# Expert products of two blocks interleaved over two PSUM banks

## The chip, the cores and the metric

The kernel runs on one core of a Trainium2 chip. The metric is the device time of one execution in microseconds; the time of a kernel is the median of its runs. The engines are TensorE (PE; its weight loads are shown apart as PEld), VectorE (DVE), ScalarE (ACT), GpSimd (POOL) and SyncE (SP), which here issues most of the transfers between HBM and the on-chip memory. PSUM is the memory that the matmuls write: eight banks, each of which takes one result of 128x512 float32.

## What is computed

A two-layer transformer block in float32 over 256 tokens and 256 context tokens. Each layer is a mixing part (a long convolution, a Fourier mix and differential attention) and then a feed-forward part with 16384 small experts, of which each token uses 128. The change is in that last part:

```python
def peer(t, wq, keys, u, v):
    ...                                        # top-k over 8 heads gives indices idx and gates g
    def chunk(args):
        tc, ic, gc = args
        hid = jnp.einsum('td,tkd->tk', tc, u[ic])
        return jnp.einsum('tk,tkd->td', gc * jax.nn.gelu(hid, approximate=False), v[ic])
```

Layer 0 runs it for 512 tokens, layer 1 for 256. Every `u` and `v` has 16384 rows of 1024.

## The kernel before

**Dense experts.** The kernel does not gather the experts of a token. It goes over all 16384 in 128 blocks of 128 and takes a gate of zero for those that a token does not use. For a block `b` it forms the hidden values of 128 experts for all `n` tokens (the hidden product, `u` transposed times the tokens), applies Gelu, multiplies by the gates, and adds the product with the block's 128 rows of `v` (the value product) onto sums that stay in PSUM over all 128 blocks. In layer 0, 384 tokens are done in this way; the other 128 tokens' rows are gathered by POOL with indirect transfers and summed on DVE (`junk`, lines 1067, and `acc`, 1077), four 128x1024 rows of each pass per pair of blocks, into a pool `row` of three buffers. In layer 1 all 256 tokens are done densely.

**Split floats.** Each float32 operand is split into two float32r parts (line 105, `split`): ACT casts it to the high part (`wh`, `vh`, `ah`), DVE subtracts that and writes the low part (`wl`, `vl`, `al`). `mm3` (line 100) then issues three matmuls, high times high, high times low and low times high. A hidden product is 8 chunks of 1024 / 128 times three matmuls, 24 in all, into one PSUM bank. A value product is, for each 128 tokens `tt` and each half (512) of the 1024 columns, three matmuls.

**Pairs.** Blocks go in pairs (`SB = 2`). `stage1` makes a block's gated hidden values (`a`, then `ah` and `al`), `stage2` splits the pair's rows of `v` and issues the value products of both blocks. In program order, hidden products of a pair stand ahead of the value products of the pair before it, so PE alternates: hidden of pair k, values of pair k-1, hidden of k+1, values of k. The accumulators `pacc` take 2n/128 banks, one for each `tt` and half: six in layer 0, four in layer 1. The value loop before is half by half, and in a half over `tt`, with both blocks in the innermost loop: six matmuls into one bank, then the next.

**Prefilled blocks.** 32 blocks of each layer (blocks 0 and 1 of every eight) have their hidden values made earlier, beside the routing, and stored in HBM (`Hd`). For these pairs `stage1` only loads `a` from `Hd`. PE then has no hidden products for that pair, and the value products of two pairs stand back to back. This comes up 15 times in each layer, and once more behind the last pair. It is called a crossing below.

**Buffers.** `vh` and `vl` have four buffers each, one for each half and block of a pair; `wh` and `wl` have three, `ha` (the tile `a`) three, the raw tiles `w` six and `wv` three.

**What sets the order.** The tile framework reorders the instructions of each engine by its own estimate of when they become ready, within the data's dependencies; on the chip each engine then runs its queue in order, and waits at semaphores. The sums over gathered rows are pinned to program order among themselves.

The names above are those in the rows and in the profile: `pm` and `pa` are PSUM tiles, `th` and `tl` the tokens' two parts, `gt` the gates.

Of the kernel before, what the change touches and what calls it, by code (L numbers as in the profile page):

```python
# [9 lines left out]
F32 = mybir.dt.float32  # L10
# [11 lines left out]
P = 128  # L22
L = 256
NT = 512
NG = 128
# [24 lines left out]
def tile_dit(ctx, tc, A, out, dbg=None):  # L50
# [36 lines left out]
    def pmt(shape=(P, 512)):  # L87
        return pm.tile(list(shape), F32, tag="pm", name=nm("pm"))
# [49 lines left out]
    def wraw(src):  # L138
        w = w4.tile([P, 1024], F32, tag="w4", name=nm("w4"))
        nc.sync.dma_start(w, src)  # L140
        return w

    def wsplit(src, eng=None):
        hi = whp.tile([P, 1024], F32R, tag="wh", name=nm("wh"))
        lo = whp.tile([P, 1024], F32R, tag="wl", name=nm("wl"))
        split(hi, lo, src, eng)
        return hi, lo
# [605 lines left out]
    def exact(o, w, xf):  # L753
        for c in range(8):
            mm(o, w[:, c * P:(c + 1) * P], xf[:, c], c == 0, c == 7)

    def hidden(l, n, b, th, tl, xf=None):
        w = wraw(A["u"][l, b])
        ps = pmt()
        if xf is not None:  # L760
            exact(ps[:, :n], w, xf)
        else:
            uh, ul = wsplit(w)
            for c in range(8):
                cs = slice(c * P, (c + 1) * P)
                mm3(ps[:, :n], uh[:, cs], ul[:, cs], th[:, c, :n], tl[:, c, :n], c == 0, c == 7)
        a = scope["ha"].tile([P, 512], F32, tag="a", name=nm("a"))
        S.activation(a[:, :n], ps[:, :n], AF.Gelu)
        return a

    NPRE = (32, 32)
    HEAD_FILLS = ((0, 1, 1, 1, 2, 2, 2, 8), (0, 1, 1, 1, 1, 1, 1, 8))
# [4 lines left out]

    def prefill(l, n, npre, th, tl, xf, Hd):
        for k in range(npre):
            a = hidden(l, n, PRE_BLOCK[l][k], th, tl, xf)  # L780
            nc.scalar.dma_start(Hd[k, :, :n], a[:, :n])
            yield

    def experts(l, n, npre, th, tl, Gd, Hd, acc, hook):
        nq = n // 32
        pacc = [pat() for _ in range(4)] + [pmt() for _ in range(n // P * 2 - 4)]
        gt = [None]

        def stage1(b):
            if b % GB == 0:  # L790
                gt[0] = b16t((P, 16, GB, 32), name="gt")
                nc.sync.dma_start(gt[0][:, :nq], Gd[:, :nq, b:b + GB, :])
            if b in PRE_BLOCK[l]:
                k = PRE_BLOCK[l].index(b)
                a = scope["ha"].tile([P, 512], F32, tag="a", name=nm("a"))
                nc.sync.dma_start(a[:, :n], Hd[k, :, :n])
            else:
                a = hidden(l, n, b, th, tl)
            a3 = a[:, :n].rearrange("p (q k) -> p q k", k=32)
            V.tensor_tensor(a3, a3, gt[0][:, :nq, b % GB], ALU.mult)  # L800
            ah, al = tagged("ah", F32R, 4), tagged("al", F32R, 4)
            split(ah[:, :n], al[:, :n], a[:, :n])
            return ah, al

        def stage2(b0, blocks):
            ws = []
            for i in range(SB):
                w = scope["ex"].tile([P, 1024], F32, tag="wv", name=nm("wv"), bufs=3)
                nc.sync.dma_start(w, A["v"][l, b0 + i])
                ws.append(w)  # L810
            vs = {}
            for half in range(2):
                for i in range(SB):
                    vh, vl = tagged("vh", F32R, 4), tagged("vl", F32R, 4)
                    split(vh, vl, ws[i][:, half * 512:(half + 1) * 512])
                    vs[half, i] = vh, vl
            end = b0 + SB == P
            for half, tt in ([(h, t) for t in range(n // P) for h in range(2)] if end else
                             [(h, t) for h in range(2) for t in range(n // P)]):
                ts = slice(tt * P, (tt + 1) * P)  # L820
                for i, (ah, al) in enumerate(blocks):
                    vh, vl = vs[half, i]
                    mm3(pacc[tt * 2 + half], ah[:, ts], al[:, ts], vh, vl, b0 == 0 and i == 0, end and i == SB - 1)

        prev = None
        for b0 in range(0, P, SB):
            cur = [stage1(b0 + i) for i in range(SB)]
            if prev is not None:
                stage2(b0 - SB, prev)
            prev = cur  # L830
            hook(b0 // SB)
        stage2(P - SB, prev)

        def result(s):
            rows = []
            for tt in range(2 * s, min(2 * s + 2, n // P)):
                y = scope["ex"].tile([P, 1024], F32, tag="wv", name=nm("y"), bufs=3)
                S.copy(y[:, 0:512], pacc[tt * 2])
                V.tensor_copy(y[:, 512:1024], pacc[tt * 2 + 1])
                rows.append(y)  # L840
            if len(rows) < 2:
                rows.append(acc[:, 0:2].rearrange("p a b -> p (a b)"))
            return rows

        return result
# [375 lines left out]
```

## Time and profile before

| | |
|---|---|
| median of 3 runs | 3024.02 us (3019.01 to 3027.01) |
| profiled execution | 3018.95 us, span 3017.2 us |
| mean granted clock of TensorE | 0.978 of full speed |
| PE, PEld busy | 2864.0 us (95%), 2435.9 us (81%) |
| DVE, ACT, POOL busy | 2223.2 us (74%), 1247.6 us (41%), 700.7 us (23%) |
| expert stage of layer 0 | 875 to 1860 us of the span |
| expert stage of layer 1 | 2380 to 3017 us of the span |

Busy time of PE counts a matmul from its start to its modelled end, and matmuls overlap; the distance between two starts says what one costs. On ACT and DVE, too, an instruction can begin some 0.08 us before the modelled end of the one ahead of it. A wait is put down to the releaser that came last.

### The profile page before, as it was taken

How to read it: one execution, taken by the hardware profiler on the slowest of the kernel's cores; microseconds unless marked ns; L12 is line 12 of the kernel's file. 1: busy time of each engine (PE TensorE's matmuls, PEld its weight loads, DVE VectorE, ACT ScalarE, POOL GpSimd, SP SyncE). 2: the span in 40 equal slices, each digit the busy share in tenths (PEclk: the TensorE clock that was granted, in tenths of full speed). 3: DMA queues.
4: the chain of work that ended last, by engine and by line, in shares of the span. 5: the costliest groups of instructions: out<-in, count | busy, mean ns of one | idle time of the engine just before them, and what ended most of it. 6: DMA issues, size and time to landing. Idle time of an engine off the chain costs nothing.

```text
span 3017.2 us, 43660 instructions
## 1 busy us (share of the span) xinstructions
PE 2864.0 (95%) x15976; PEld 2435.9 (81%) x15976; DVE 2223.2 (74%) x4464; ACT 1247.6 (41%) x2294; POOL 700.7 (23%) x609
## 2 busy tenths in 40 slices
PE   6889999999989999999999999899799999999999
PEld 2678778776667888888898897788788898899888
DVE  7766786797977887888887787746688657765665
ACT  3334565421443333333333334336414455555554
POOL 4544433430013333333333332300200000000000
PEclk8899999999999999999999999999999999999999
DMA  7323555233788898889888885225457977766662
GB/s 261 108 97 116 175 180 220 101 114 105 278 332 326 315 326 300 307 318 323 312 317 300 307 312 186 81 97 176 165 162 250 331 249 243 259 223 223 221 224 103
DMA packets 234536, 682.19 MB, mean 226 GB/s; under 512 B 21956, under 2 KB 92682, under 8 KB 231120
## 3 DMA queue, kind: packets, MB, share of 16 engines
q1 hardware_dynamic: 172080, 505.48, 48.4%
q0 software_dynamic: 38928, 140.35, 13.1%
q10 hardware_dynamic: 23312, 33.56, 3.1%
q8 instruction: 125, 2.05, 0.3%
q14 instruction: 91, 0.75, 0.1%
HBM read 612.20 MB, written 67.11 MB: 225 GB/s over the span
## 4 chain that ended last, share of the span: by engine, by line
PE 52%; issue 15%; DVE 14%; DMA 13%; POOL 4%; ACT 2%; POOLq 0%; DVEq 0%; SPq 0%; ACTq 0%
PE pm L98 32%; PE pa L98 19%; DMA row<-in_ug_dram,ix 7%; DMA row<-in_v_dram,ix 4%; DVE og L734 3%; POOL row L1049 2%; DVE wl L110 1%; DVE oa L730 1%; DVE junk L171 1%; DVE acc L1077 1%; DVE junk L1067 1%; DVE vl L110 1%; POOL qt L466 0%; DMA a<-Hd 0%; POOL pr L167 0%
## 5 line engine op out<-in xcount | busy, mean ns | idle before, releaser
L98 PE MATMUL pm<-th,wh 128*128 128x256 f32 (+2 forms) x1680 | 532.4, 317 | 2.3 <-DVE th L241 2.3
L98 PE MATMUL pm<-tl,wh 128*128 128x256 f32 (+2 forms) x1680 | 530.2, 316 | 3.3 <-DVE tl L242 3.2
L98 PE MATMUL pm<-th,wl 128*128 128x256 f32 (+2 forms) x1680 | 529.7, 315 | 0.7 <-DVE wl L110 0.7
L106 ACT CAST wh<-w 128x1024 fp32r<-128x1024 f32 x328 | 343.0, 1047 | 409.3 <-PE pm L98 351.1
L110 DVE TENSOR_TENSOR wl<-w,wh 128x1024 fp32r<-128x1024 f32 x312 | 392.5, 1259 | 161.5 <-ACT wh L106 160.7
L98 PE MATMUL pa<-vl,ah 128*128 128x512 f32 x1024 | 406.1, 397 | 26.5 <-DVE vl L110 26.5
L110 DVE TENSOR_TENSOR vl<-wv,vh 128x512 fp32r<-128x512 f32 x512 | 339.1, 687 | 119.2 <-ACT vh L106 113.6
L106 ACT CAST vh<-wv 128x512 fp32r<-128x512 f32 x512 | 305.3, 619 | 265.4 <-PE pm L98 86.0
L98 PE MATMUL pa<-vh,ah 128*128 128x512 f32 x1024 | 402.5, 394 | 5.1 <-ACT vh L106 5.1
L98 PE MATMUL pa<-vh,al 128*128 128x512 f32 x1024 | 403.7, 394 | 0.3 <-DVE al L110 0.3
L98 PE MATMUL pm<-acc,w 128*128 128x256 f32 (+1 forms) x1280 | 355.6, 427 | 8.6 <-ACT acc L1011 8.6
L98 PEld LDWEIGHTS pm<-tl,wh 128*128 128x128 f32 x1680 | 320.9, 191 | 13.6 <-DVE tl L242 4.5
L98 PEld LDWEIGHTS pm<-th,wh 128*128 128x128 f32 x1680 | 321.0, 191 | 11.8 <-DVE th L241 2.9
L98 PEld LDWEIGHTS pm<-th,wl 128*128 128x128 f32 x1680 | 320.8, 191 | 5.4 <-DVE wl L110 0.9
L106 ACT CAST ah<-a 128x384 fp32r<-128x384 f32 (+1 forms) x256 | 117.7, 460 | 439.5 <-DVE a L800 399.6
L98 PEld LDWEIGHTS pm<-acc,w 128*128 128x128 f32 x1280 | 235.8, 191 | 78.0 <-ACT acc L1011 9.0
L1049 POOL DMA_INDIRECT row<-in_ug_dram,ix x128 | 165.3, 1291 | 507.7 <-DVE junk L1067 298.5
L98 PEld LDWEIGHTS pa<-vl,ah 128*128 128x128 f32 x1024 | 194.7, 190 | 70.5 <-DVE vl L110 32.7
L1049 POOL DMA_INDIRECT row<-in_v_dram,ix x128 | 170.6, 1332 | 311.5 <-DVE acc L1077 279.3
L98 PEld LDWEIGHTS pa<-vh,ah 128*128 128x128 f32 x1024 | 194.5, 190 | 44.8 <-ACT vh L106 6.3
L98 PEld LDWEIGHTS pa<-vh,al 128*128 128x128 f32 x1024 | 194.7, 190 | 41.1 <-DVE al L110 0.8
L1077 DVE SCALAR_TENSOR_TENSOR acc<-row,gg,acc 128x1024 f32<-128x1024 f32 x127 | 162.8, 1282 | 62.7 <-DMA row<-in_v_dram,ix 61.8
(309 smaller groups left out, 5292.5 us busy)
## 6 DMA issues: line engine op xcount, KB each, us to landing
w<-in_u_dram SPq DMA_DIRECT2D x256, 512.0 KB, 4.2
wv<-in_v_dram SPq DMA_DIRECT2D x256, 512.0 KB, 4.9
w<-in_w_ada_dram SPq DMA_DIRECT2D x96, 512.0 KB, 4.3
w<-in_w_in_dram SPq DMA_DIRECT2D x88, 512.0 KB, 3.8
Gd<-st SPq DMA_DIRECT2D x18, 2048.0 KB, 7.2
gt<-Gd SPq DMA_DIRECT2D x16, 1536.0 KB, 10.6
w<-in_wq_dram SPq DMA_DIRECT2D x32, 512.0 KB, 3.6
gt<-Gd SPq DMA_DIRECT2D x16, 1024.0 KB, 6.7
```

Source lines behind the costliest of these rows:

```text
L98: T.matmul(o, l, r, start=start, stop=stop, skip_group_check=True)
L106: S.copy(hi, src)
L110: (eng or V).tensor_tensor(lo[:, ks], src[:, ks], hi[:, ks].bitcast(F32), ALU.subtract)
L171: i = V.scalar_tensor_tensor(slot((P, 1024), BF16, "junk"), w, 1.0, sil[:, s], op0=ALU.mult, op1=ALU.mult, accum_out=m)
L730: V.tensor_tensor(oa, row(0), iob, ALU.is_equal)
L734: V.tensor_tensor(og[:, w * HG:(w + 1) * HG], oa, gv[:, w * HG:(w + 1) * HG, None].to_broadcast([P, HG, P, 2]), ALU.mult)
L1049: nc.gpsimd.indirect_dma_start(out=r, out_offset=None, in_=src, in_offset=bass.IndirectOffsetOnAxis(ap=ix, axis=0))
L1067: pin(V.scalar_tensor_tensor(slot((P, 1024), BF16, "junk"), r, 1.0, ta, op0=ALU.mult, op1=ALU.mult, accum_out=hg[:, k:k + 1]))
L1077: pin(V.scalar_tensor_tensor(ta, r, gg[:, k:k + 1], ta, op0=ALU.mult, op1=ALU.add))
```

## The change

The hidden products of a pair are issued together by `hidden_pair`: for each chunk and each of the three parts, first the matmul of one block, then that of the other, so that consecutive matmuls write two PSUM banks in turn. Both Gelus stand behind the pair. Prefilled blocks keep the old form (`hidden`). In `stage2` the loop over `tt` is now outermost and the two halves are innermost: for each block and each of the three parts, a matmul into the bank of half 0, then one into that of half 1. The numbers of matmuls, weight loads, casts, subtractions and transfers stay the same.

```diff
-    def hidden(l, n, b, th, tl, xf=None):
...
+    def hidden_pair(l, n, b, th, tl):
+        us = [wsplit(wraw(A["u"][l, b + i])) for i in range(SB)]
+        ps = [pmt() for i in range(SB)]
+        for c in range(8):
+            cs = slice(c * P, (c + 1) * P)
+            for k, (w, t) in enumerate(((0, th), (0, tl), (1, th))):
+                for i in range(SB):
+                    mm(ps[i][:, :n], us[i][w][:, cs], t[:, c, :n], c == 0 and k == 0, c == 7 and k == 2)
+        return [gelu(n, p) for p in ps]
...
+        def raw(b0):
+            if b0 not in PRE_BLOCK[l]:
+                return hidden_pair(l, n, b0, th, tl)
+            r = []
+            for i in range(SB):
+                a = scope["ha"].tile([P, NT - NG], F32, tag="a", name=nm("a"))
+                nc.sync.dma_start(a[:, :n], Hd[PRE_BLOCK[l].index(b0 + i), :, :n])
+                r.append(a)
+            return r
+
+        def stage1(b, a):
...
-            for half, tt in ([(h, t) for t in range(n // P) for h in range(2)] if end else
-                             [(h, t) for h in range(2) for t in range(n // P)]):
+            for tt in range(n // P):
                 ts = slice(tt * P, (tt + 1) * P)
                 for i, (ah, al) in enumerate(blocks):
-                    vh, vl = vs[half, i]
-                    mm3(pacc[tt * 2 + half], ah[:, ts], al[:, ts], vh, vl, b0 == 0 and i == 0, end and i == SB - 1)
+                    for k, (a, w) in enumerate(((ah, 0), (ah, 1), (al, 0))):
+                        for half in range(2):
+                            mm(pacc[tt * 2 + half], a[:, ts], vs[half, i][w], b0 == 0 and i == 0 and k == 0,
+                               end and i == SB - 1 and k == 2)
...
-            cur = [stage1(b0 + i) for i in range(SB)]
+            cur = [stage1(b0 + i, a) for i, a in enumerate(raw(b0))]
```

Three places in the built programs. The first is PE's queue in layer 1 at a crossing, where the value products of one pair end and those of the next begin; `vh_22999` and `vh_23003` are half 0 of the next pair's two blocks, `vh_23007` is half 1 of its first block. Before:

```order
L98 MATMUL pa_21762<-vl_22952,ah_22811 128x512
L98 MATMUL pa_21762<-vh_22951,al_22812 128x512
L98 MATMUL pa_21759<-vh_22999,ah_22893 128x512
L98 MATMUL pa_21759<-vl_23000,ah_22893 128x512
L98 MATMUL pa_21759<-vh_22999,al_22894 128x512
L98 MATMUL pa_21759<-vh_23003,ah_22931 128x512
L98 MATMUL pa_21759<-vl_23004,ah_22931 128x512
L98 MATMUL pa_21759<-vh_23003,al_22932 128x512
```

and of the changed kernel:

```order
L98 MATMUL pa_21761<-vh_22943,al_22812 128x512
L98 MATMUL pa_21762<-vh_22951,al_22812 128x512
L98 MATMUL pa_21759<-vh_22999,ah_22926 128x512
L98 MATMUL pa_21759<-vl_23000,ah_22926 128x512
L98 MATMUL pa_21759<-vh_22999,al_22927 128x512
L98 MATMUL pa_21760<-vh_23007,ah_22926 128x512
L98 MATMUL pa_21759<-vh_23003,ah_22931 128x512
L98 MATMUL pa_21759<-vl_23004,ah_22931 128x512
L98 MATMUL pa_21759<-vh_23003,al_22932 128x512
L98 MATMUL pa_21760<-vl_23008,ah_22926 128x512
```

Half 1 of the first block is used by the fourth matmul of the pair, where it was used by the thirteenth. The second place is ACT's queue at the same crossing; `ah_22984` and `ah_22986` are the cast of the first prefilled block behind it. Before:

```order
L106 CAST vh_22999<-wv_22995 128x512
L106 CAST ah_22931<-a_22928 128x256
L106 CAST vh_23003<-wv_22997 128x512
L106 CAST ah_22984<-a_22981 128x256
L106 CAST vh_23007<-wv_22995 128x512
L106 CAST ah_22991<-a_22988 128x256
L106 CAST vh_23011<-wv_22997 128x512
```

and now:

```order
L106 CAST vh_22999<-wv_22995 128x512
L106 CAST vh_23003<-wv_22997 128x512
L106 CAST ah_22986<-a_22979 128x256
L106 CAST vh_23007<-wv_22995 128x512
L106 CAST vh_23011<-wv_22997 128x512
```

The order of the four casts is the same, and one cast of a prefilled block still stands ahead of half 1. The third place is DVE's queue in layer 0, in the pairs that have no sums for the modulation in them: the four sums over gathered rows of one pair (`junk`), the low parts `wl`, the gates `a` and the low parts `al`. Before:

```order
L1067 SCALAR_TENSOR_TENSOR junk_11394,gg_4629<-row_11392,acc_4582 128x1024
L1067 SCALAR_TENSOR_TENSOR junk_11398,gg_4629<-row_11396,acc_4582 128x1024
L1067 SCALAR_TENSOR_TENSOR junk_11402,gg_4629<-row_11400,acc_4582 128x1024
L110 TENSOR_TENSOR wl_11450<-w_2384_11446,wh_11449 128x1024
L800 TENSOR_TENSOR a_11291<-a_11291,gt_11016 128x384
L1067 SCALAR_TENSOR_TENSOR junk_11406,gg_4629<-row_11404,acc_4582 128x1024
L110 TENSOR_TENSOR al_11295<-a_11291,ah_11294 128x384
L110 TENSOR_TENSOR wl_11656<-w_2437_11652,wh_11655 128x1024
```

and now:

```order
L1078 SCALAR_TENSOR_TENSOR junk_11394,gg_4629<-row_11392,acc_4582 128x1024
L1078 SCALAR_TENSOR_TENSOR junk_11398,gg_4629<-row_11396,acc_4582 128x1024
L1078 SCALAR_TENSOR_TENSOR junk_11402,gg_4629<-row_11400,acc_4582 128x1024
L1078 SCALAR_TENSOR_TENSOR junk_11406,gg_4629<-row_11404,acc_4582 128x1024
L110 TENSOR_TENSOR wl_11417<-w_2380_11414,wh_11416 128x1024
L810 TENSOR_TENSOR a_11322<-a_11322,gt_11020 128x384
L810 TENSOR_TENSOR a_11324<-a_11324,gt_11020 128x384
L110 TENSOR_TENSOR wl_11655<-w_2437_11652,wh_11654 128x1024
```

The fourth sum stood behind a `wl` and an `a` and now follows the third at once; both gate products come behind it. In the changed kernel four sums stand in a row in this way 26 times, before not once; in the pairs with sums for the modulation, `junk wl a junk al junk wl a junk` has become three sums, `wl`, both `a`, and the fourth sum.

## Rows read from the trace of the kernel before

**Rows 1.** The two expert stages by window: us, busy us of PE, PEld, DVE, ACT, POOL, PEclk.

```profile
875.00:1860.00 985.00, 953.16 (x4660) 847.91 (x4659) 780.34 (x1178) 349.00 (x590) 332.42 (x254) 0.98 0.87 310
...
2380.00:3017.00 637.00, 630.02 (x3860) 566.66 (x3858) 400.38 (x665) 321.70 (x579) 0.00 (x0) 1.00 0.65 224
```

**Rows 2.** Timeline of PE in layer 1: start us, us, engine, line, what.

```profile
2600.72 0.28 PE L98 MATMUL pm<-th,wh 128*128 128x256 f32 x1
...
2606.35 0.28 PE L98 MATMUL pm<-th,wl 128*128 128x256 f32 x1
2606.47 0.40 PE L98 MATMUL pa<-vh,ah 128*128 128x512 f32 x1
...
2611.71 0.39 PE L98 MATMUL pa<-vh,al 128*128 128x512 f32 x1
2611.94 0.39 PE L98 MATMUL pa<-vh,ah 128*128 128x512 f32 x1
2612.16 0.39 PE L98 MATMUL pa<-vl,ah 128*128 128x512 f32 x1
...
2617.15 0.39 PE L98 MATMUL pa<-vh,al 128*128 128x512 f32 x1
```

**Rows 3.** Timeline of PE among the float16 products of the routing.

```profile
761.59 0.40 PE L98 MATMUL pa<-ob,og 128*128 128x128 f16 x4 [0.28 <-DVE og L734]
761.83 1.50 PE L98 MATMUL pm<-acc,w 128*128 128x384 f32 x4
```

**Rows 4.** Groups by form in layer 1's expert stage: busy us, mean ns | idle before.

```profile
L110 DVE TENSOR_TENSOR vl<-wv,vh 128x512 fp32r<-128x512 f32 x255 | 172.1, 689 | 92.5 <-ACT vh L106 87.2
L106 ACT CAST vh<-wv 128x512 fp32r<-128x512 f32 x255 | 154.8, 620 | 131.6 <-PE pa L98 77.0 <-DMA wv<-in_v_dram 37.2 <-issue 13.5
...
L110 DVE TENSOR_TENSOR wl<-w,wh 128x1024 fp32r<-128x1024 f32 x96 | 117.5, 1224 | 116.6 <-ACT wh L106 116.4
L106 ACT CAST wh<-w 128x1024 fp32r<-128x1024 f32 x96 | 100.4, 1046 | 85.7 <-PE pm L98 77.2 <-DMA w<-in_u_dram 8.4
...
L800 DVE TENSOR_TENSOR a<-a,gt 128x256 f32<-128x256 f32 x128 | 52.5, 417 | 7.2 <-DMA a<-Hd 3.7 <-ACT a L768 3.5
L106 ACT CAST ah<-a 128x256 fp32r<-128x256 f32 x128 | 52.0, 406 | 87.1 <-DVE a L800 75.7 <-PE pa L98 11.0
L768 ACT ACTIVATE a<-pm 128x256 f32<-128x256 f32 x98 | 37.1, 379 | 3.9 <-PE pm L98 3.9
```

**Rows 5.** Waits of PE, then of DVE, in layer 0: us, times, longest us.

```profile
PE pa L98 <- DVE vl L110: 26.5, 14, 4.2
...
DVE junk L1067 <- DMA row<-in_ug_dram,ix: 66.9, 38, 4.3
DVE acc L1077 <- DMA row<-in_v_dram,ix: 61.8, 43, 3.9
DVE a L800 <- DMA a<-Hd: 34.1, 16, 16.1
```

**Rows 6.** Timeline of DVE in layer 0, around one block's sums over gathered rows.

```profile
1172.44 0.08 DVE L1067 DVE_READ_ACCUMULATOR junk<-row,acc 128x1 f32 x1
...
1174.97 1.22 DVE L110 TENSOR_TENSOR wl<-w,wh 128x1024 fp32r<-128x1024 f32 x1
1176.11 0.55 DVE L800 TENSOR_TENSOR a<-a,gt 128x384 f32<-128x384 f32 x1
1178.68 1.23 DVE L1067 SCALAR_TENSOR_TENSOR junk<-row,acc 128x1024 bf16<-128x1024 f32 x1 [2.02 <-DMA row<-in_ug_dram,ix]
...
1179.83 0.56 DVE L110 TENSOR_TENSOR al<-a,ah 128x384 fp32r<-128x384 f32 x1
```

**Rows 7.** Timeline of POOL, the gather that the wait at 1178.68 waited for.

```profile
1172.79 1.81 POOL L1049 DMA_INDIRECT row<-in_ug_dram,ix  x1 [3.00 <-DVE junk L1067]
```

**Rows 8.** DMA issues in layer 0's expert stage: median us from issue to landing.

```profile
row<-in_ug_dram,ix POOLq DMA_INDIRECT x123, 6.5
```

**Rows 9.** One window of layer 0 by engine, columns as in Rows 1.

```profile
1187.00:1191.20 4.20, 3.82 (x10) 3.06 (x11) 4.20 (x8) 0.84 (x2) 0.00 (x0) 0.59 1.05 371
```

More of the change, by code (lines that the diff above doesn't have):

```diff
@@ L755, in exact, with gelu @@
             mm(o, w[:, c * P:(c + 1) * P], xf[:, c], c == 0, c == 7)
-    def hidden(l, n, b, th, tl, xf=None):
[L758 to L766, printed above, removed]
+    def gelu(n, ps):
         a = scope["ha"].tile([P, 512], F32, tag="a", name=nm("a"))
@@ L769, in hidden @@
         return a
+    def hidden(l, n, b, xf):
+        ps = pmt()
+        exact(ps[:, :n], wraw(A["u"][l, b]), xf)
+        return gelu(n, ps)
+    def hidden_pair(l, n, b, th, tl):
[7 more added lines that the diff above has]
+        return [gelu(n, p) for p in ps]
     NPRE = (32, 32)
@@ L779, in prefill @@
         for k in range(npre):
-            a = hidden(l, n, PRE_BLOCK[l][k], th, tl, xf)
+            a = hidden(l, n, PRE_BLOCK[l][k], xf)
             nc.scalar.dma_start(Hd[k, :, :n], a[:, :n])
@@ L787, in experts @@
         gt = [None]
-        def stage1(b):
+        def raw(b0):
[8 more added lines that the diff above has]
+        def stage1(b, a):
             if b % GB == 0:
@@ L792, in stage1 @@
                 nc.sync.dma_start(gt[0][:, :nq], Gd[:, :nq, b:b + GB, :])
[L793 to L798, printed above, removed]
             a3 = a[:, :n].rearrange("p (q k) -> p q k", k=32)
```

## The prediction

> **What bounds the kernel now.** I read the stages by window first, then PE's timeline inside them, then the waits of PE and DVE, then the groups by form. The two expert stages take 985 and 637 us of the 3017 us span, and PE is busy in 953 and 630 us of them [rows 1]. The change touches these two stages; everything ahead of them and between them is left as it is.
>
> Whether a matmul can become cheaper is read from starts, not from busy time. In layer 1, 24 value matmuls lie between 2611.71 and 2617.15 us: 5.44 us, 0.2267 us each [rows 2]. The granted clock there is 1.00, the 2.4 GHz level [rows 1], at which 512 columns take 0.2133 us, so 13.3 ns are paid on top. The 48 hidden matmuls from 2600.72 to 2606.35 (47 distances, 5.63 us) stand 0.1198 us apart for 256 columns (0.1067 us): 13.1 ns again. The overhead is per matmul and fixed.
>
> The two layers differ in what stands beside PE. In layer 1 DVE is busy 401 of 637 us, and PE all but 7. In layer 0 DVE is busy 780 of 985 us and waits for 205 us; 129 us of these waits are for gathered rows, 34 us for stored hidden values, and PE's own wait is 26.5 us, all of it for DVE's `vl` [rows 1, 5]. So layer 1 runs at PE's pace, and layer 0 at PE's and DVE's in turn.
>
> **Two banks in turn: 0 us.** 4608 matmuls of layer 0 (2304 hidden, 2304 value) and 3840 of layer 1 (2304 and 1536) change their order. The kernel before already changes banks after every sixth value matmul, so the trace has the case that the change makes common. The matmul at 2611.94 writes another bank than the one at 2611.71 and starts 0.23 us after it; the next writes the same bank and starts 0.22 us later [rows 2]. Hidden to value at 2606.47 is another bank too, 0.12 us after the matmul before, as within the bank. Had the bank cost the 13 ns, such a start would come at 0.21 and 0.11 us. A second row speaks against it: four float16 matmuls of 128 columns, all into one bank and accumulating in pairs, take 0.24 us, 60 ns each [rows 3], 7 ns over their 53. Accumulating in one bank is thus possible with less, and the 13 ns go with the operands' kind or their weight loads. Neither changes. Bounds: 0, and, if float32r in turn reached what float16 pays, (13.3 - 6.7) ns x 8448 = 56 us gained. I take 0, since float32r rows stand nearest.
>
> The Trainium skill, TensorE: Matmul & The Clock Gate, section Back-to-back issue gap, gives an isolated gap of columns / 2.4 + 2.5 ns. By it the whole 10.8 ns would be there to win, 91 us; the trace disagrees at every bank change shown above.
>
> **Hidden products side by side: 0 us.** Both blocks' splits are needed at the start, where the second had half a pair's time left. Between two hidden phases lie 24 value matmuls, 5.4 us in layer 1 and more in layer 0; the second split takes a cast and a subtraction, 1.05 + 1.22 us [rows 4], and fits. Without that cover each pair would pay 2.3 us. Both Gelus (2 x 0.38 us) come at the end of the pair; their results are used a whole hidden phase later, except at a crossing.
>
> **Values with the halves inside: +18 us in layer 1.** The four buffers of `vh` and `vl` used to come free in two steps: half 0 in the middle of a value phase, half 1 at its end. Now all four are read until the last `tt`. The first block's half 0 is last read eight matmuls before the end, the second block's by the last but one. Where a hidden phase follows, the four casts (4 x 0.62) and subtractions lie beside it (5.6 us) and cost nothing. At a crossing nothing covers them. Take the first planned start of the next pair as 0. The second block's half 0 is free at about 0 (last but one matmul starts at -0.45 and ends 0.39 later). ACT's queue is then: that cast 0.62, the prefilled block's `ah` 0.41, the first block's half 1 0.62 [rows 4], done at 1.65, with a handover some 1.7. PE's fourth matmul wants that tile at 3 x 0.2267 = 0.68, so PE stands 1.0 us. DVE must do `wl`, two `a`, `wl`, two `al` and one `a` from the end of the hidden phase on, about 5.2 us after a first cast of 1.05, and then `vl`, so that it arrives within a few tenths of the same point; I add 0.1 us. 16 crossings x 1.1 = 18 us. Bounds: 0, if the casts run early enough, and 16 x 2.5 = 40 us, if `vl` of all four tiles (4 x 0.69) had to pass first.
>
> **DVE's order in layer 0: +32 us.** A gathered row has three buffers. In the rows shown, the sum that frees a buffer ends at 1172.52, POOL starts the next gather at 1172.79, and the sum that needs it can start at 1178.68, 6.2 us later [rows 6, 7]; with the median landing of 6.5 us and the 0.27 us before it, the mean is some 6.7 [rows 8]. So the fourth sum of a pair may start no earlier than 6.7 us after the end of its first, and what stands between them on DVE is no loss. From start to start, a sum takes 1.15 to 1.27 us (1178.68 to 1179.83, and its read-out), a `wl` 1.14 (1174.97 to 1176.11) and an `a` about 0.48. Before, a pair without modulation has two sums, a `wl` and an `a` there: 4.1 us, wait 2.6. Now it has two sums: 2.5 us, wait 4.2. A pair with modulation had two sums, two `wl`, two `a` and an `al`, 6.2 us, wait 0.5; now two sums, a `wl` and two `a`, 4.6 us, wait 2.1. The 16 prefilled pairs change little (two sums and two `vl` of 0.6, 3.7 us, were between; now two sums, an `a` and an `al`, 3.5: 3.0 to 3.2 us of wait). Sum before: 27 x 2.6 + 21 x 0.5 + 16 x 3.0 = 129 us, just what the waits show [rows 5]. Now: 26 x 4.2 + 22 x 2.1 + 16 x 3.2 = 207 us, 78 more. DVE's queue is in order, so what waits behind the fourth sum waits too: the other `wl`, `al` and the four `vl`, and PE for these.
>
> What of the 78 us reaches the end? The other 76 us of DVE's waits (205 - 129) shrink as it becomes the later engine: about 25 us at the start (one wait of 16.1 [rows 5]) and the end of the stage stay, up to 50 can go, since a `vl` that comes late finds its cast done, and the load of the second prefilled block now stands behind `vl`. DVE's sum is then 780 + 207 + 25 = 1012 us at least and 780 + 207 + 76 = 1063 at most, against 985: +27 to +78. I take +32, near the lower end, because a late DVE finds everything else ready. The lower bound of the change is below nothing: with a reload of 5.5 us the same sum gives 130 us of waits, no more than now, and PE's 26.5 us could go.
>
> **The sum.** 0 + 0 + 18 + 32 = +50 us on 3018.95 us of the profiled execution (span 3017.2), 3069. The median of the runs shown is 5 us above that execution, so I forecast 3074 us.
>
> **Rivals.** (1) Layer 0 absorbs its row waits: only the crossings of layer 1 are paid, 3024 + 18 = 3042. For it: DVE's share of 780 in 985 us leaves slack. Against: its waits are almost all for rows that now come later still. (2) The other side: the loads of stored hidden values were the cause of layer 0's stalls. Before, the second prefilled `a` waits for its load ahead of `vl`, and PE behind it [rows 5]; now `vl` stand ahead. If rows then come early enough, that is if the reload stays under about 5.5 us, PE's 26.5 us go, and with them the low clock behind the longest of these stalls (1.9 us each [rows 9], for five of them 10 us), and 18 us are paid in layer 1: 3024 - 36 + 18 = 3006. (3) The banks matter after all, by 6.6 ns: 25 us in layer 1, none in layer 0 as long as DVE bounds it: 3074 - 25 = 3049; if it does not, 3024 - 56 + 18 = 2986. (4) Layer 0 is dearer: its stalls grow past the length at which the clock falls. In the 4.2 us from 1187 us, where one of these stalls ends, the granted clock is 0.59, between its levels of 1.2 and 2.4 GHz, and 10 matmuls start in place of 18, 1.9 us lost [rows 9]. Sixteen more of these, and waits for loads that stay: 3074 + 30 = 3104, up to 3130. (5) Turning through banks makes PE pause so often that the clock falls in every value phase, by eight matmuls' worth (1.6 us) in each of 128 phases: 3074 + 205 = 3280. Against it, the clock is 1.00 in layer 1, where banks already change every six matmuls. The Trainium skill, same page, section A second HAM failure mode: psum-queue depth-cycling, tells of such a kernel.
>
> **How the numbers follow.** Forecast 0.60; rival 1 0.14; rival 2 0.05; rival 3 0.04; rival 4 0.13; rival 5 0.02; no difference that shows, 0.02. The forecast's own range is 3050 to 3095. Up to 3120 rival 4 is mostly in; down to 3034 rival 1. A measurement of this kernel tells about 0.3% (9 us) from no change. Faster by more: rival 2 and half of rival 3, 0.07. Within: 0.02 and the low end of rival 1, 0.07 in all. Slower: 0.86.
>
> **What would show it.** PE's starts in layer 1: 0.227 and 0.120 us apart as before (0.213 and 0.107 would make rival 3). At each of the 16 crossings of layer 1 a wait of about 1 us on PE ended by ACT's `vh` or DVE's `vl`, where there was none. In layer 0 DVE's waits for rows near 200 us in place of 129, with DVE's other waits smaller, and a stage of about 1017 us. If the stage of layer 1 is not longer, the crossing was misread; if layer 0's waits for rows have not grown, the order of the sums does not decide.

## The result and the profile after

The changed kernel takes 3061.97 us (median of 4 runs, 3058.19 to 3064.52), the kernel before in the same job 3024.14 us (3019.01 to 3027.01): a ratio of 1.0126, 95% interval 1.0107 to 1.0145. It is slower by 37.8 us; the forecast was 3074, its own range 3050 to 3095. The profiled execution took 3064.21 us (span 3062.4). That of the kernel before took 3018.95 us, at the fast end of its runs, so the two profiles differ by 45 us, 7 more than the medians; the differences of stages below are parts of these 45.

The two expert stages by window, with columns as in [rows 1]: us, busy us of PE, PEld, DVE, ACT, POOL, PEclk. Each window begins and ends as far from the stage as in [rows 1].

```profile
872.50:1901.40 1028.90, 970.09 (x4660) 855.53 (x4659) 780.75 (x1178) 342.14 (x590) 329.25 (x254) 0.97 0.84 297
2419.80:3062.20 642.40, 633.36 (x3861) 563.29 (x3859) 387.07 (x665) 313.47 (x577) 0.00 (x0) 1.00 0.65 222
```

Layer 0 is 44 us longer (1028.9 against 985), layer 1 5.4 us; the stretch between the stages is 1.6 us shorter. DVE's work in layer 0 is the same, 780 us; it waits 44 us more. The tables below measure a stage from its first hidden matmul to the start of its last value matmul: layer 0 974.2 before and 1018.1 now, layer 1 627.7 and 633.4.

PE's timeline in layer 1, against [rows 2] (x2 is two matmuls in one row):

```profile
2427.13 0.63 PE L98 MATMUL pa<-vh,ah 128*128 128x512 f32 x2
2427.60 0.62 PE L98 MATMUL pa<-vl,ah 128*128 128x512 f32 x2
2428.06 0.62 PE L98 MATMUL pa<-vh,al 128*128 128x512 f32 x2
...
2432.14 0.61 PE L98 MATMUL pa<-vh,al 128*128 128x512 f32 x2
2432.60 0.40 PE L98 MATMUL pm<-th,wh 128*128 128x256 f32 x2
...
2436.67 0.40 PE L98 MATMUL pm<-th,wl 128*128 128x256 f32 x2
```

From 2427.13 to 2432.14 lie 22 distances between value matmuls, 0.228 us each, and from 2432.60 to 2436.67 34 between hidden ones, 0.120 us each: those of before within 1 ns.

The waits of PE and then of DVE in layer 0, against [rows 5]: us, times, longest.

```profile
PE pa L98 <- ACT vh L106: 35.4, 14, 8.4
PE pm L98 <- DVE wl L110: 14.6, 5, 3.4
PE pa L98 <- DVE vl L110: 8.6, 16, 3.0
...
DVE acc L1088 <- DMA row<-in_v_dram,ix: 84.0, 39, 5.9
DVE junk L1078 <- DMA row<-in_ug_dram,ix: 81.9, 40, 4.9
DVE a L810 <- DMA a<-Hd: 61.5, 17, 15.4
```

In the kernel before, PE waited for ACT's `vh` too, beside the `vl` of [rows 5]:

```profile
PE pa L98 <- ACT vh L106: 5.1, 2, 4.1
```

PE waits 58.6 us where it waited 31.6. DVE's waits for rows grew from 128.7 to 165.9 us, by half of the 78 forecast; its waits for stored hidden values grew too, from 34.1 to 61.5, where the prediction had them shrink. How the first kind reaches PE is seen in DVE's queue ahead of a stall at 1721.58:

```profile
1711.03 2.61 DVE L1088 SCALAR_TENSOR_TENSOR acc<-row,gg,acc 128x1024 f32<-128x1024 f32 x2 [1.11 <-DMA row<-in_v_dram,ix]
1716.75 2.70 DVE L1088 SCALAR_TENSOR_TENSOR acc<-row,gg,acc 128x1024 f32<-128x1024 f32 x2 [3.12 <-DMA row<-in_v_dram,ix]
1719.37 1.02 DVE L810 TENSOR_TENSOR a<-a,gt 128x384 f32<-128x384 f32 x2
1720.30 1.22 DVE L110 TENSOR_TENSOR wl<-w,wh 128x1024 fp32r<-128x1024 f32 x1
```

and on PE:

```profile
1721.58 0.44 PE L98 MATMUL pm<-th,wl 128*128 128x384 f32 x1 [3.39 <-DVE wl L110]
```

Of four sums in a row, the first and the third wait for a row (1.11 and 3.12 us), and `wl` stands behind them and both gates; PE's hidden phase stops on it. Inside hidden phases there were no such stalls before; now there are five, of 2.5 to 3.6 us, 15.5 us together. The second kind, at the longest stall, in DVE's queue:

```profile
1812.51 1.28 DVE L1088 SCALAR_TENSOR_TENSOR acc<-row,gg,acc 128x1024 f32<-128x1024 f32 x1 [1.12 <-DMA row<-in_v_dram,ix]
1813.71 1.02 DVE L110 TENSOR_TENSOR al<-a,ah 128x384 fp32r<-128x384 f32 x2
...
1815.12 1.22 DVE L110 TENSOR_TENSOR wl<-w,wh 128x1024 fp32r<-128x1024 f32 x1
1825.01 0.56 DVE L810 TENSOR_TENSOR a<-a,gt 128x384 f32<-128x384 f32 x1 [8.68 <-DMA a<-Hd]
...
1826.71 2.50 DVE L110 TENSOR_TENSOR vl<-wv,vh 128x512 fp32r<-128x512 f32 x4
```

and in SP's queue of transfers:

```profile
1805.69 0.42 SPq L801 DMA_DIRECT2D a<-Hd  x1
1814.29 0.33 SPq L801 DMA_DIRECT2D a<-Hd  x1
```

The load of a pair's second stored block is issued at 1814.29, just when the first of the two `al` is done and gives its `a` buffer free (three buffers). Both Gelus now come at the end of a pair, so this `al` comes late, here behind a sum that itself waited. The gate that needs the load starts 10.7 us after its issue, and `al`, `vl` and PE (8.4 us) wait.

The largest part of PE's waits, though not of their growth, is at the crossings: 27.8 us, against 21.6 before. The cause there has changed. Before, at most of them, `vl` stood on DVE behind the gate of the pair's second stored block, and that gate waited for its load:

```profile
1186.17 0.56 DVE L800 TENSOR_TENSOR a<-a,gt 128x384 f32<-128x384 f32 x1 [1.91 <-DMA a<-Hd]
```

Now, at twelve crossings (24.0 of the 35.4 us), ACT's casts `vh` stand behind the cast `ah` of the first stored block. That cast waits for a gate on DVE, and the gate stands behind a sum that waited for its row. One of them, on DVE, ACT and PE:

```profile
1431.47 1.29 DVE L1088 SCALAR_TENSOR_TENSOR acc<-row,gg,acc 128x1024 f32<-128x1024 f32 x1 [5.93 <-DMA row<-in_v_dram,ix]
...
1435.88 1.02 DVE L110 TENSOR_TENSOR al<-a,ah 128x384 fp32r<-128x384 f32 x2
1436.83 0.55 DVE L810 TENSOR_TENSOR a<-a,gt 128x384 f32<-128x384 f32 x1
...
1437.45 0.51 ACT L106 CAST ah<-a 128x384 fp32r<-128x384 f32 x1 [2.07 <-DVE a L810]
1437.87 2.17 ACT L106 CAST vh<-wv 128x512 fp32r<-128x512 f32 x4
...
1438.54 0.49 PE L98 MATMUL pa<-vh,ah 128*128 128x512 f32 x1 [2.05 <-ACT vh L106]
```

So of the 27 us by which PE's waits grew, 14.6 came inside hidden phases, 8.4 in the one stall behind a late stored block and 6.2 at crossings; elsewhere, mostly at the start of the stage, PE waits some 2 us less.

### The profile page after: what moved, and what is told of

Same layout as the page of the kernel before. It is cut to its first block, busy times and chain, and to the rows that moved or that the text cites. A ratio compares the mean times of both kernels' runs of the same rounds, so it can differ in the third digit from the quotient of the medians.

```text
span 3062.4 us, 43628 instructions
## 1 busy us (share of the span) xinstructions
PE 2878.7 (94%) x15976; PEld 2435.2 (80%) x15976; DVE 2211.7 (72%) x4464; ACT 1232.9 (40%) x2294; POOL 698.6 (23%) x609
## 4 chain that ended last, share of the span: by engine, by line
PE 47%; issue 17%; DMA 15%; DVE 13%; POOL 5%; ACT 2%; POOLq 0%; SPq 0%; DVEq 0%; ACTq 0%
PE pm L98 30%; PE pa L98 17%; DMA row<-in_v_dram,ix 6%; DMA row<-in_ug_dram,ix 6%; DVE og L734 3%; POOL row L1060 2%; DVE wl L110 2%; DVE oa L730 1%; DMA a<-Hd 1%; DVE acc L1088 1%; DVE junk L171 1%; POOL qt L466 0%; DMA w<-in_u_dram 0%; POOL pr L167 0%; DVE ob L731 0%
## 5 line engine op out<-in xcount | busy, mean ns | idle before, releaser
L98 PE MATMUL pm<-th,wl 128*128 128x256 f32 (+2 forms) x1680 | 410.2, 317 | 15.2 <-DVE wl L110 15.2
L98 PE MATMUL pm<-th,wh 128*128 128x256 f32 (+2 forms) x1680 | 410.8, 318 | 2.3 <-DVE th L241 2.3
L98 PE MATMUL pm<-tl,wh 128*128 128x256 f32 (+2 forms) x1680 | 409.1, 317 | 2.5 <-DVE tl L242 2.5
L98 PE MATMUL pa<-vh,ah 128*128 128x512 f32 x1024 | 331.6, 400 | 35.4 <-ACT vh L106 35.4
L106 ACT CAST vh<-wv 128x512 fp32r<-128x512 f32 x512 | 289.3, 618 | 180.5 <-PE pa L98 93.4
L98 PE MATMUL pa<-vl,ah 128*128 128x512 f32 x1024 | 335.9, 400 | 11.7 <-DVE vl L110 11.7
L98 PE MATMUL pa<-vh,al 128*128 128x512 f32 x1024 | 329.8, 395 | 0.0
L98 PEld LDWEIGHTS pm<-th,wl 128*128 128x128 f32 x1680 | 290.1, 192 | 21.6 <-DVE wl L110 17.0
L98 PEld LDWEIGHTS pm<-th,wh 128*128 128x128 f32 x1680 | 293.9, 192 | 15.7 <-DVE th L241 2.9
L98 PEld LDWEIGHTS pm<-tl,wh 128*128 128x128 f32 x1680 | 289.5, 192 | 9.1 <-DVE tl L242 3.9
```

The costliest lines, as they stand in the source:

```text
L98: T.matmul(o, l, r, start=start, stop=stop, skip_group_check=True)
L106: S.copy(hi, src)
```

## The experiments

Twelve kernels. Ratios are to the kernel before, run with them on the same chip; stages in us as defined above. A stage length is that of one profiled execution, while runs of one kernel lie up to 21 us apart (the kernel before, 17 runs in one job: 3010 to 3031). A difference of a few us between two lengths of layer 0 therefore shows nothing by itself. Layer 1 repeats better: 626.1 to 627.7 in the four kernels with the old order of both products.

| kernel | median | ratio, interval | layer 0 | layer 1 |
|---|---|---|---|---|
| before | 3024.14 | 1 | 974.2 | 627.7 |
| changed | 3061.97 | 1.0126 [1.0107, 1.0145] | 1018.1 | 633.4 |
| values_only | 3041.34 | 1.0073 [1.0046, 1.0100] | 992.4 | 642.4 |
| hidden_only | 3087.02 | 1.0230 [1.0211, 1.0249] | 1035.6 | 635.4 |
| before_nosum | 2977.13 | 0.9868 [0.9850, 0.9885] | 928.6 | 626.7 |
| after_nosum | 2996.22 | 0.9926 [0.9907, 0.9944] | 940.0 | 635.5 |
| after_nosum_ha4 | 2980.27 | 0.9861 [0.9833, 0.9889] | 934.7 | 631.9 |
| after_row4 | 3017.85 | 0.9992 [0.9974, 1.0011] | 966.9 | 637.2 |
| after_ha4 | 3047.24 | 1.0104 [1.0079, 1.0129] | 990.2 | 632.1 |
| after_row4_ha4 | 3006.65 | 0.9952 [0.9933, 0.9971] | 949.1 | 631.4 |
| before_row4_ha4 | 2999.89 | 0.9943 [0.9922, 0.9964] | 954.0 | 626.4 |
| after_split | 3090.31 | 1.0233 [1.0202, 1.0264] | 1038.9 | 636.3 |
| before_row4_ha4_split | 3031.85 | 1.0034 [1.0018, 1.0051] | 978.9 | 626.1 |
| values_tt_row4_ha4 | 2994.60 | 0.9913 [0.9885, 0.9941] | 941.2 | 626.0 |

**values_only.** The kernel before with the changed loop of the value product:

```
-            for half, tt in (...):
-                ... mm3(pacc[tt * 2 + half], ...)
+            for tt in range(n // P):
+                ... for half in range(2):
+                        mm(pacc[tt * 2 + half], a[:, ts], vs[half, i][w], ...)
```

> Only the value products are changed (halves innermost), the hidden products stay one block after the other. Theory (order of the row sums on DVE): four sums stand in a row 8 times here, against 26 in the changed kernel and none before; a walk through DVE's order with a reload of 6.5 us gives 139 us of waits for rows against 114 before and 184 in the changed kernel, so layer 0 takes about 25/70 of its 44 us, +16; layer 1 takes +4 (15 crossings of 0.26 us). 3024 + 20 = 3044 us, DVE's waits for rows in layer 0 near 142. Rival (value buffers held to the end of the phase are the cost): all of it is here, 3062 us, with rows waited for as before (129).

Measured 3041.34 us, layer 0 +18, waits for rows 142 us, in all 3 us under the theory's time. Layer 1 is +14.7 where +4 was expected: one stall of 4.2 us with a stretch of half-speed starts behind it, at a crossing where a gate (2433.61) waited 4.3 us for its stored block, and dearer crossings. The rival, that the held buffers are the whole cost of layer 0, falls.

**hidden_only.** The changed kernel with the old loop of the value product:

```
-            for tt in range(n // P):
-                ... for half in range(2): mm(pacc[tt * 2 + half], ...)
+            for half, tt in (...):
+                ... mm3(pacc[tt * 2 + half], ...)
```

> Only the hidden products are changed (two blocks side by side), the value products keep the halves outside. Theory (order of the row sums on DVE): four sums stand in a row 43 times; the same walk gives 216 us of waits for rows against 114 before and 184 in the changed kernel. Layer 0 is 44 us longer or more, up to 64; layer 1 as before within 2 us. 3070 to 3088 us. Rival (value buffers held to the end of the phase): nothing is held here, 3024 us within 5.

Measured 3087.02 us, layer 0 +61. The waits in layer 0:

```profile
DVE acc L1087 <- DMA row<-in_v_dram,ix: 99.1, 41, 5.0
DVE junk L1077 <- DMA row<-in_ug_dram,ix: 97.3, 42, 5.0
...
PE pm L98 <- DVE wl L110: 24.7, 19, 3.0
```

196 us for rows, and 19 waits inside hidden phases. So the cost of layer 0 comes with the hidden products side by side, which the prediction put at nothing by themselves and charged to DVE's order. With the new value loop beside them the kernel is 25 us faster (3061.97); why is not shown. Layer 1 was to stay within 2 us and is 7.7 longer: a late stored block (3.1 us at 2995.68) and some 0.3 us at each crossing, where an `ah` cast that waits for its buffer stands ahead of half 1's casts. The two halves of the change do not add up (18 + 61 against 44 in layer 0), so no share of the 44 us can be given to either.

**before_nosum and after_nosum.** The gathers and their sums are left out of both kernels:

```
-            for k in range(4 * (sb % 32), 4 * (sb % 32) + 4):
+            if sb == 32:
+                S.activation(hg, gg, AF.Gelu)
+                V.tensor_scalar(ta, ta, hg[:, 0:1], None, op0=ALU.mult)
+            for k in ():
```

> The kernel before, with the 256 gathers of rows and their 256 sums on DVE left out of layer 0 (so the share of the gathered experts is missing from the output). Both theories: layer 0 falls from 974 us to PE's pace, about 948 us (2304 x 0.1733 + 2304 x 0.2267 = 921.6 plus stalls ahead of it, at crossings and at the start), 3024 - 26 = 2998 us. It is the base for the next run.

> The changed kernel with the same 256 gathers and sums left out. Theory (row sums): its layer 0 is within 10 us of the run without sums of the kernel before, its layer 1 5.7 us longer as measured; 2998 + 6 to 16 = 3004 to 3014 us. Rival (buffers held, or stored hidden values loaded late): the 44 us of layer 0 stay, 2998 + 44 + 6 = 3048 us.

Measured 2977.13 us (21 under the expected: the stalls I left in layer 0 went too) and 2996.22 us. Layer 0's difference shrinks from 43.9 to 11.4 us: by the profiles, 32.5 us of it hang on the sums. By the medians it is less, since the change costs 37.8 us with the sums and 19.1 without. The theory is missed by little (11.4 us where at most 10 were expected, and 19.1 in all where 6 to 16 were); the rival, that the 44 us stay, falls. Half of what is left is one stall of 5.5 us, at 1752.28, behind a stored block for which a gate waited 9.4 us.

**after_nosum_ha4.** The same with a fourth buffer for `a` (and `a`, `ah`, `al` cut to their 384 used columns, as in the runs below):

```
-        pools(es, f"p{l}", ha=3)
+        pools(es, f"p{l}", ha=4)
```

> The changed kernel with the 256 gathers and sums left out and a fourth buffer for hidden values. Theory (what is left of the change without the sums is the late load of stored hidden values, and the crossings): layer 0 falls from 940 us to 931 us (928.6 in the kernel before without sums), layer 1 from 635.5 to 631 us; 2996 - 9 - 5 = 2982 us, 3 to 8 us over the kernel before without sums. Rival (the crossings or the two banks cost the rest): 2993 us or more.

Measured 2980.27 us, layer 0 934.7 and layer 1 631.9. The fourth buffer takes 5.3 us from layer 0 and 3.6 from layer 1. What remains over before_nosum (6.1 and 5.2 us) is small delays among the value matmuls, mostly at crossings, and the start of the stage. The medians, of two different jobs, differ by only 3.1 us and the profiles by 4.8, less than the two stages together, since in this profile the stretch between the stages, which no edit touches, is 6.7 us shorter, for a reason not looked for.

**after_row4, after_ha4, after_row4_ha4.** The changed kernel with more buffers, one kind each and both:

```
-            r = ...tile([P, 1024], F32, tag="row", ..., bufs=3)
+            r = ...tile([P, 1024], F32, tag="row", ..., bufs=4)
-        pools(es, f"p{l}", ha=3)
+        pools(es, f"p{l}", ha=4)
```

> The changed kernel with a fourth buffer for gathered rows (room for it by cutting the tiles a, ah and al from 512 to the 384 columns that are used). The sums stand as bunched as before the edit (four in a row 45 times), only their wait for the reload goes: by the walk with 6.5 us a reload, 184 us of waits for rows become 12. Theory (reload time): layer 0 falls from 1018 us to between 940 us, the length without sums, and 955; in all 2996 to 3012 us. Rival (the bunch itself, 5 us of sums ahead of wl and al, delays PE without any wait): layer 0 stays over 1000 us, 3045 us or more.

> The changed kernel with a fourth buffer for hidden values a (same tile cut), three for rows as they are. Theory (rows cost 33 of layer 0's 44 us, stored hidden values that are loaded late cost the rest): DVE's waits for Hd in layer 0 fall from 61 to 30 us or less and the single waits of 3 us and 8 us on PE go; layer 0 1005 to 1012 us, layer 1 from 633 to 630 us; 3062 - 6 to 16 = 3046 to 3056 us. Rival (the late loads are the main cost and the row waits follow from them): layer 0 980 us or less, 3020 us.

> Both edits on the changed kernel. Theory: layer 0 near 932 us (without sums and without late loads), layer 1 630 us; 2996 - 8 - 5 = 2983 us, up to 2995. Rival (value buffers held to the end still cost in layer 0): over 3010 us.

Layer 0 falls by 51 us with the fourth row buffer, though the sums stand more bunched than before it (four in a row 45 times, against 26): the rival, the bunch itself, falls. It was to reach 955 and stays at 967; the whole, 3017.85 us, is above the 2996 to 3012 expected and level with the kernel before. Its waits:

```profile
DVE a L810 <- DMA a<-Hd: 63.3, 17, 16.2
...
DVE junk L1078 <- DMA row<-in_ug_dram,ix: 21.6, 15, 3.5
...
DVE acc L1088 <- DMA row<-in_v_dram,ix: 19.6, 13, 3.1
```

41 us for rows against the 12 of the walk, which knows no reload longer than 6.5 us. On the whole these reloads were no longer than that (median landing 6.3 us), but single ones took up to 12.6 us, and a walk with one fixed reload leaves those out. The fourth `a` buffer alone gives 3047.24 us, as expected, but takes 28 us from layer 0 in the profile where 6 to 13 were expected. That profile is of the fastest of the four runs; the ratios to the kernel before (1.0104 against 1.0126) have overlapping intervals, so this buffer's worth alone is not shown. The profile has

```profile
DVE junk L1078 <- DMA row<-in_ug_dram,ix: 90.7, 34, 5.9
DVE acc L1088 <- DMA row<-in_v_dram,ix: 87.6, 38, 5.4
DVE a L810 <- DMA a<-Hd: 16.0, 2, 15.9
```

that is more waits for rows than the changed kernel has (178 against 166), and yet a shorter stage. Layer 1's single stall goes with it, as in every run with four `a` buffers. Both together: layer 0 949, layer 1 631, 3007 us; the expected 2983 to 2995 were missed. Layer 0 was to be near 932 and keeps 36 us of waits for rows.

**before_row4_ha4.** Both edits on the kernel before.

> Both edits on the kernel before. Theory: layer 0 falls from 974 us to near 932 us, as without the sums; layer 1 627 us; 2980 us, up to 2990, and 3 to 10 us under the changed kernel with the same edits (the crossings of layer 1). Rival (in the kernel before DVE is late for other reasons than rows): no gain beyond the 7 us, 3012 us.

Measured 2999.89 us, 10 over the upper end, layer 0 954. With four buffers of each kind no cost of the change shows in layer 0 (949.1 against 954.0; the profile of the changed one is of the fastest of its eight runs, 7.7 us under their median), and 5.0 us in layer 1. In all it is 6.8 us slower by the medians, and the two intervals overlap.

**after_split.** The changed kernel with two of a pair's sums ahead of its value splits:

```
+            hook(b0 // SB, 0)
             if prev is not None:
                 stage2(b0 - SB, prev)
             prev = cur
-            hook(b0 // SB)
+            hook(b0 // SB, 1)
```

> The changed kernel with two of the four gathers and sums of a pair issued ahead of its value splits and two behind them; buffers, products and the number of sums as in the changed kernel. Four sums in a row stand nowhere any more (26 times in the changed kernel); the walk with 6.5 us a reload gives 118 us of waits for rows, against 184 in the changed kernel and 114 before. Theory (the order of the sums): layer 0 falls from 1018 us to 985 to 990 us, the late stored hidden values stay; 3062 - 28 to 33 = 3029 to 3034 us, with DVE's waits for rows near 130 us. Rival (the two blocks side by side need both wl at the start, whatever the sums do): 3055 us or more.

A miss, and the most telling: 3090.31 us, layer 0 21 us longer than the changed kernel's, with 53 us less of waits for rows (112.5):

```profile
DVE acc L1089 <- DMA row<-in_v_dram,ix: 62.5, 28, 5.0
DVE junk L1079 <- DMA row<-in_ug_dram,ix: 50.0, 22, 4.6
...
PE pa L98 <- DVE vl L110: 60.2, 17, 5.3
```

One of the 17, first on DVE and then on PE:

```profile
1070.57 1.22 DVE L1079 SCALAR_TENSOR_TENSOR junk<-row,acc 128x1024 bf16<-128x1024 f32 x1 [2.06 <-DMA row<-in_ug_dram,ix]
...
1071.72 0.69 DVE L110 TENSOR_TENSOR vl<-wv,vh 128x512 fp32r<-128x512 f32 x1
```

```profile
1072.46 0.80 PE L98 MATMUL pa<-vl,ah 128*128 128x512 f32 x1 [2.86 <-DVE vl L110]
```

The sums now stand right ahead of the `vl` that PE wants next: in 15 of the 17 a sum that waited 1.8 to 5.0 us for its row stands ahead of that `vl`, with at most two instructions between. Four sums in a row occur nowhere any more. So neither the sum of DVE's waits nor how often four sums stand in a row sets the cost; what stands behind a waiting sum, and how soon PE wants it, does. The rival as it was put (both `wl` at the start) did not show either: no wait on PE for `wl` is left here.

**before_row4_ha4_split.** The same edit on before_row4_ha4.

> The kernel before with four buffers for rows and for hidden values, and two of the four sums of a pair ahead of its value splits. Theory: the 40 us of waits for rows that four buffers left shrink, since no three sums stand in a row; layer 0 from 954 to 940 us, 2986 us. Rival (what is left comes from stored hidden values that are loaded late, 57 us of DVE's waits): 3000 us, no change from four buffers alone.

Also a miss: 3031.85 us, though waits for rows fell from 40 to 25 us; layer 0 is 25 us longer, with PE's waits for `vl` at 29.2 us (13.8 without the split). The reason is the same: at each of the 14 longer ones a sum is the instruction just ahead of the `vl`, and 13 of these sums had waited for their row.

**values_tt_row4_ha4.** before_row4_ha4 with banks in turn, halves outside, `tt` innermost:

```
+            for half in range(2):
+                for i, (ah, al) in enumerate(blocks):
+                    for k, (a, w) in enumerate(((ah, 0), (ah, 1), (al, 0))):
+                        for tt in range(n // P):
+                            mm(pacc[tt * 2 + half], a[:, tt * P:(tt + 1) * P], vs[half, i][w], ...)
```

> The kernel before with four buffers for rows and for hidden values, and value products that change the bank with every matmul (two banks in turn in layer 1, three in layer 0) but keep the halves outside, so that the value buffers come free as before or earlier. Theory (the overhead of a float32r matmul is fixed): starts 0.227 us apart, layer 1 626 to 628 us, in all 3000 us within 6. Rival (banks in turn are worth 6.6 ns or more a matmul): layer 1 616 us or less and 2990 us or less. Rival (banks in turn lower the clock): layer 1 above 640 us.

Measured 2994.60 us, as the theory has it, layer 1 626.0 (626.4 without the turns). PE's timeline there, and the stage by window:

```profile
2371.45 0.61 PE L98 MATMUL pa<-vh,ah 128*128 128x512 f32 x2
2371.90 0.62 PE L98 MATMUL pa<-vl,ah 128*128 128x512 f32 x2
...
2373.71 0.62 PE L98 MATMUL pa<-vh,al 128*128 128x512 f32 x2
```

```profile
2350.60:2986.00 635.40, 629.21 (x3860) 566.82 (x3859) 398.39 (x665) 323.20 (x578) 0.00 (x0) 1.00 0.68 224
```

Ten matmuls in 2.26 us: 0.226 us each, at a clock of 1.00. Both rivals on the banks fall. Layer 0 is 941 us, 13 less than with the old order; it has the lowest median of all kernels that compute the whole, 0.9% under the kernel before. The two runs were in different jobs and their intervals overlap, so how much of the 13 us is this order is open.

## Why the prediction was right, and where its sizes were off

Right in sign and place, and the sum is near, but its nearness is luck: layer 0 was put 12 us too low (+32, in the profiles 43.9) and layer 1 12 us too high (+18, measured 5.7), and the two errors cancel. Point by point:

**Two banks in turn, 0 us:** confirmed, by the unchanged distances of the changed kernel and by values_tt_row4_ha4, which turns banks without holding buffers. The isolated gap of 2.5 ns that the Trainium skill gives (TensorE: Matmul & The Clock Gate, Back-to-back issue gap) does not show for these float32r matmuls: 13 ns stand at every change of bank, as within one. The float16 reading of 60 ns was taken at the end of a group; along the routing 1200 starts lie 57 ns apart, 3.7 over the 53.3, so the bound of 56 us for that case should have been 81. Neither was gained. Rivals 3 and 5 are out: the clock of layer 1 is 1.00 in both kernels with banks in turn.

**Hidden products side by side, 0 us:** right as far as the matmuls go. As an edit, it is the half of the change that costs layer 0 more (hidden_only +61, values_only +18), through what it does to DVE's queue and to the release of `a`.

**Values with the halves inside, +18 us in layer 1:** too dear. Layer 1 lost 5.7 us, 3.25 of it in one stall behind a late stored block, the rest mostly at crossings, 0.18 to 0.30 us at each of 15. At this one 48 value matmuls from 2488.92 to 2499.82 take 10.90 us, where 47 distances of 0.2267 make 10.65. The step that failed is "the second block's half 0 is free at about 0", and with it the 1.7 us. ACT and then PE at this crossing, which begins at 2494.39:

```profile
2493.00 1.14 ACT L106 CAST vh<-wv 128x512 fp32r<-128x512 f32 x2 [0.82 <-PE pa L98]
2494.05 0.40 ACT L106 CAST ah<-a 128x256 fp32r<-128x256 f32 x1
2494.36 1.14 ACT L106 CAST vh<-wv 128x512 fp32r<-128x512 f32 x2
```

```profile
2493.94 0.62 PE L98 MATMUL pa<-vh,al 128*128 128x512 f32 x2
2494.39 0.39 PE L98 MATMUL pa<-vh,ah 128*128 128x512 f32 x1
...
2495.11 0.66 PE L98 MATMUL pa<-vh,ah 128*128 128x512 f32 x2
```

ACT's order is as forecast, two casts, `ah`, two casts. But both half 0 casts are done by 2494.14, while the second block's own half 0 is read until the first matmul of 2493.94 ends, at 2494.33. So the second cast must have had another buffer, by the times that of the first block's half 1, which is last read five matmuls earlier. The buffer went to the tile that asked next, not to the same tile of the next pair. So the third cast ends 0.6 us after the crossing begins, not 1.7, and the fourth matmul (2495.11) is not late.

**DVE's order in layer 0, +32 us:** the mechanism holds, in that sums which wait hold up what stands behind them, and the size was 43.9 us in the profiles. The part that hangs on the sums is 32.5 us by the profiles (43.9 less the 11.4 without them) and 19 us by the medians. But two steps inside it were wrong, with opposite signs. "207 us of waits for rows" became 166. The reload was shorter than the 6.7 us put in: with the changed kernel's median landing of 5.9 us and the same 0.27 ahead of it, the prediction's own sum gives some 173 us, an estimate. And "the other 76 us of DVE's waits shrink" failed: they are 82 us. The waits for stored blocks grew by 27 us, while the rest did shrink, from 42 to 21. I had put the release of `a` at no cost, having looked only at the Gelus' results ("used a whole hidden phase later") and not at the third buffer that they hold until then. The range +27 to +78 held since it was wide, not because the split of it was right. Nor was the way to PE all there: the prediction has PE wait for DVE's `wl`, `al` and `vl`, and reads its waits before as "all of it for DVE's `vl`", where 5.1 us more were for ACT's `vh`. Now 35.4 us are for `vh`, most of them through ACT's queue at the crossings of layer 0, for which it had no term. Nor would the sum of waits have been a sound measure: after_split has fewer waits for rows than the kernel before (112 against 129) and loses 65 us in layer 0, after_ha4 has more than the changed kernel and a shorter layer 0 in its profile. No run keeps DVE's old order of sums beside the new hidden products, so how much of the cost is that order, and how much the later `wl`, gates and `al` themselves, stays open.

**The low clock (rival 4)** took little. Of PE's starts in layer 0, distances over the pace (columns at 2.4 GHz and 13.3 ns) by more than 0.42 us sum to 66.4 us now and 33.9 before; those of 0.15 to 0.42 us, nearly all of them where the trace has the granted clock at half, as behind the stall in [rows 9], to 16.3 and 13.4; smaller ones to 14.2 and 5.7. So 32 of the 44 us are stalls themselves and 3 the low clock behind them.

Of rival 2, that `vl` ahead of the second stored block frees PE, one half came: PE's waits for `vl` fell from 26.5 to 8.6 us. But the sums and the later loads took their place. Rival 1, nothing lost in layer 0, is out.

## What to carry to other kernels

Side by side in one phase means that both results are released at its end; count the buffers of everything that is read behind it, and the loads that wait for those buffers, before calling the reordering free. A wait in an in-order queue costs what stands behind it: ask for each wait which instruction follows and when the bottleneck engine wants that, since the sum of waits can fall while the time rises. Where a reload was hidden by nothing, one more buffer was worth more here than either order of its readers that was tried: with four of each, both kernels beat the kernel before by 0.5%, and the change no longer shows in layer 0.

## What was not expected of the hardware

How long a gathered row takes to land varies more than the walk with a fixed reload allowed for. The medians of the two passes are 5.8 and 5.9 us in the changed kernel, 6.5 and 6.2 in the kernel before, 6.5 and 6.3 in after_row4, 6.1 and 6.1 in after_row4_ha4, and 6.9 and 7.2 in before_row4_ha4. In the changed kernel only a quarter of the landings could be told. Within one run the spread is wider than between runs: 4.3 to 12.6 us in after_row4. The number of row buffers does not set the median, since the kernels with four lie on both sides of the kernel before. The loads of `w` move roughly with the rows (4.7 us in after_ha4, whose rows take 5.9 and 6.0; 5.2 before; 5.7 in after_row4_ha4; 6.3 in after_row4; 6.2 in before_row4_ha4; 4.1 in after_nosum, where there are no gathers). That would fit traffic that both share, but no run separates this from other causes.
